# Turning q and k two heads at a time and splitting them afterwards in a hybrid encoder layer

## The chip, the cores and the metric

The kernel runs on one core of one Trainium2 chip. The time is the device time of one execution in microseconds (us); three runs of the kernel before gave 1966.2 to 1967.8 us, with a median of 1966.9 us. The engines are named as in the profile: PE (TensorE), PEld (its weight loads), DVE (VectorE), ACT (ScalarE), POOL (GpSimd) and SP (SyncE, which issues all DMA transfers of this kernel). L885 is line 885 of the kernel.

## The reference, cut to what matters

One layer of a hybrid encoder over 1024 tokens of width 1024: a gated feed-forward block, then attention beside a state-space scan, then a second feed-forward block and a gated embedding. The change touches only the way from the projected q and k to the scores of the attention:

```python
u = x @ w_in[i]
q, k, v, z, xs, bm, cm, dt_raw = jnp.split(u, SPLIT_POINTS, axis=-1)
qf = _rms(q.reshape(B, S, N_Q_HEADS, HEAD_DIM).astype(jnp.float32), q_norm[i])
kf = _rms(k.reshape(B, S, N_KV_HEADS, HEAD_DIM).astype(jnp.float32), k_norm[i])
qh = _apply_rope(qf, cos, sin).astype(x.dtype)
kh = _apply_rope(kf, cos, sin).astype(x.dtype)
...
s = jnp.einsum('bqhgd,bkhd->bhgqk', qi, k, preferred_element_type=jnp.float32) * scale
```

There are eight q heads and two k heads of 64 values each. Behind the attention's inputs come the channels of the scan (`xs`, `bm`, `cm`), which go through a five-tap convolution along the tokens, and `dt_raw`, which goes through a softplus.

## The kernel before, in words

All products keep float32 accuracy by splitting each operand into a high part in the PE's reduced float32 format and a low part, the remainder; `mm3` makes three products of the parts. The scores use the same idea in another form. A head has only 64 values, while a matmul takes 128 partitions, so the high part of a q head lies on partitions 0 to 63 of the tile `Q` and its low part on partitions 64 to 127. `K` holds, for each of the two k heads, a plane with the high part on both halves and a plane with the low part on both halves. Two matmuls of 128 partitions then make all four products of parts.

`in_proj` runs `qkv_part` and then `xbc_part`. In `qkv_part` there are eight token tiles of 128 tokens for q (`qq`, 24 matmuls of 512 columns each) and then eight tiles for k, v and dt together (`kv`, 24 matmuls of 272 columns each). Each result goes through `norm` (ACT squares, DVE sums, POOL takes the power -0.5) and `rope` (L847: a Newton step, the scaling L852, two half products L858, L859 and the sum L860, all on DVE). `step` staggers this by hand: while the product of tile t is issued, `rope` is issued for tile t-1 and the turn of tile t-3 for q. After `rope` the kernel before copies the high part on ACT (L895 for q, L878 for k), subtracts for the low part on DVE (L87, written to the tile `qs`), turns 128 tokens x 128 values with both parts of one head per transpose on PE (L901, eight per q tile; L884, four per k tile, each k part written twice for the two halves), and copies the turned tile from PSUM to `Q` (L902) or `K` (L885) on ACT.

The PE runs strictly in program order (`in_order`). The orders on the other engines and on SP's queue come from a planner that simulates the timeline with costs of its own; each engine then executes its list in order, and a waiting instruction holds what stands behind it.

PSUM is held in two pools: `sm`, four buffers of 512 values, and `big`, two of 1024. The products of q and of k, v, dt stand in `sm`; the turned q tiles of the kernel before stand in `big`, the turned k tiles in `sm`. The work tiles of `qkv_part` (`sq`, `qn`, `qs`) belong to the pool `qwork`. It is closed when `qkv_part` ends, and the pools of `xbc_part` (`xwork` with the tile `conv`, `prep`, `zwork2`, `xtab` with the convolution's table `cw`) take over its addresses.

At the end of `qkv_part` the last steps are not run at once: they are put on `self.pend`, and the first product of the convolution's channels, `xbc_gemm(0)`, made inside `qkv_part`, runs two of them after each of its two halves of 24 matmuls. Then `xbc_part` begins: `cw` is loaded (L957), the products of the channel groups j = 1, 2, ... follow, 48 matmuls each into a buffer of `big`, and each is read by `conv` (one ACT instruction at L964 that needs `cw`, four taps on DVE at L969). `ssd_prep` (L1059 on) works on dt beside it. Group j = 2 needs the `big` buffer that the convolution of group 0 reads.

Of the kernel before, what the change touches and what calls it, by code (L numbers as in the profile page):

```python
# [18 lines left out]
P = 128  # L19
# [17 lines left out]
class Layer:  # L37
# [778 lines left out]
    def qkv_part(self, c, xT):  # L816
# [30 lines left out]

        def rope(v, nh, m, ss, r, nm, t):

            self.newton(r, ss, nh)  # L850
            qn = wk.tile([P, nh, HD], F32, name="qn")
            nc.vector.tensor_tensor(out=qn, in0=v, in1=r.unsqueeze(2).broadcast_to([P, nh, HD]), op=ALU.mult)  # L852
            T1, T2 = (x[:, t] for x in T[nm])
            H2 = HD // 2
            for a in range(2):
                o = slice(a * H2, (a + 1) * H2)
                i = slice((1 - a) * H2, (2 - a) * H2)
                nc.vector.tensor_tensor(out=m[:, :, o], in0=qn[:, :, i], in1=T2[:, o].unsqueeze(1).broadcast_to([P, nh, H2]), op=ALU.mult)  # L858
            nc.vector.tensor_tensor(out=qn, in0=qn, in1=T1.unsqueeze(1).broadcast_to([P, nh, HD]), op=ALU.mult)  # L859
            nc.vector.tensor_tensor(out=qn, in0=qn, in1=m, op=ALU.add)  # L860
            return qn

        NK = NKV * HD
        late = []

        def kv_front(t, ps):
# [5 lines left out]
            return st  # L872

        def kv_back(t, st):

            kn = rope(*st, "k", t).unsqueeze(2).broadcast_to([P, NKV, 2, HD])
            kd = wk.tile([P, NKV, 2, 2, HD], F32R, name="qs", bufs=4)
            nc.scalar.copy(out=kd[:, :, 0], in_=kn)  # L878

            def turn():  # L880
                pt = self.pss().rearrange("p (g j t) -> p g j t", g=NKV, j=2)
                for g in range(NKV):
                    for j in range(2):
                        nc.tensor.transpose(out=pt[:, g, j], in_=kd[:, g, j].rearrange("p a d -> p (a d)").bitcast(F32), identity=self.ident)  # L884
                nc.scalar.copy(out=K[:, :, :, t * P:(t + 1) * P], in_=pt)  # L885
            late.append(turn)
            return kd[:, :, 1], kn, kd[:, :, 0]

# [3 lines left out]
        def q_back(t, st):  # L892
            qs = wk.tile([P, NQ, 2, HD], F32R, name="qs", bufs=4)
            qn = rope(*st, "q", t)
            nc.scalar.copy(out=qs[:, :, 0], in_=qn)  # L895

            def turn():
                pt = self.psb().rearrange("p (h t) -> p h t", t=P)
                qv = qs.bitcast(F32)
                for hh in range(NQ):  # L900
                    nc.tensor.transpose(out=pt[:, hh], in_=qv[:, hh].rearrange("p a d -> p (a d)"), identity=self.ident)  # L901
                nc.scalar.copy(out=Q[:, :, t * P:(t + 1) * P], in_=pt)  # L902
            late.append(turn)
            return qs[:, :, 1], qn, qs[:, :, 0]

        backs, los = [], []

        def step(t, ps, front, back, keep=1):


            if len(late) > keep or not front:
                late.pop(0)()
            st = front(t, ps) if front else None
            if los:
                self.lo(*los.pop())
            if backs:
                los.append(backs.pop()())
            if front:
                backs.append(lambda: back(t, st))

# [6 lines left out]
        for t in range(NT):  # L927
            ps = self.kv(t, xT)
            step(t, ps, kv_front, kv_back, 2)
            if t == 0:  # L930
                tables("k", 1.0)
        self.pend += [lambda: step(NT, None, None, None)] * 4
        self.x0 = self.xbc_gemm(0, xT, 1)
# [1025 lines left out]
```

## Time and profile before

| | us |
|---|---|
| median of three runs | 1966.9 |
| span of the profiled execution | 1962.3 |
| what lies around the span (median less span) | 4.6 |
| PE busy | 1938.6 (99%) |
| DVE busy | 1533.1 (78%) |
| ACT busy | 879.7 (45%) |
| q and k part, start of the first and of the last transpose | 720.3 and 789.5 |

The profiled execution's own time is given as its span alone; the three runs were not profiled, and the difference between their median and the span is taken for what lies around it. Times in the views are counted from the start of the span. In the timeline a row gives the start, the length, the engine, the line, the operation and, in brackets, the idle time before it and what ended it; neighbours of one kind are merged. Matmuls overlap, so a PE row is longer than the distance to the next one.

### The profile page before, as it was taken

What the parts mean: (1) busy time and instruction counts of PE and PEld (TensorE: products, weight loads), DVE (VectorE), ACT (ScalarE), POOL (GpSimd) and SP (SyncE); (2) the same over time, 40 slices, a digit from 0 to 9 for tenths busy, and PEclk for the clock granted to TensorE, in tenths of its full rate; (3) what the DMA queues carried; (4) which work ended last, traced back from release to release, by engine and by line L of the source; (5) the groups of instructions that cost most, each with busy time, mean ns of one, the idle gap of its engine ahead of it and who ended that gap; (6) DMA issues with size and microseconds to landing.
All of it is one profiled execution on the core that took longest, in us unless ns stands there. A gap on an engine that the chain in (4) does not pass through costs nothing.

```text
span 1962.3 us, 25749 instructions
## 1 busy us (share of the span) xinstructions
PE 1938.6 (99%) x9196; PEld 1614.3 (82%) x9196; DVE 1533.1 (78%) x2378; ACT 879.7 (45%) x1509; POOL 392.8 (20%) x292
## 2 busy tenths in 40 slices
PE   8999999999999999999999999999999999999998
PEld 7888888888888889888888888788888888888886
DVE  7977776867668658759998878997777777787698
ACT  7433333334444224538887775643333334443311
POOL 0144544430001132000101001003545440001011
PEclk9999999999999999999999999999999999999999
DMA  8434544559865112231003383253545439986122
GB/s 303 136 124 154 192 177 145 193 187 377 282 226 172 65 42 68 87 111 45 7 1 98 116 292 114 86 179 138 185 146 202 159 135 336 341 267 220 39 75 97
DMA packets 147180, 309.95 MB, mean 158 GB/s; under 512 B 17665, under 2 KB 30337, under 8 KB 147052
## 3 DMA queue, kind: packets, MB, share of 16 engines
q1 hardware_dynamic: 147052, 308.31, 44.9%
q8 instruction: 72, 1.18, 0.3%
q14 instruction: 56, 0.46, 0.1%
HBM read 216.83 MB, written 91.42 MB: 157 GB/s over the span
## 4 chain that ended last, share of the span: by engine, by line
PE 90%; DVE 6%; DMA 1%; POOL 1%; issue 1%; ACT 1%; SPq 0%; DVEq 0%; ACTq 0%; POOLq 0%
PE sm L122 56%; PE big L508 12%; PE sm L508 9%; PE big L122 3%; PE big L1151 2%; PE sm L1173 2%; DVE nm L1158 1%; PE sm L1188 1%; PE sm L1189 1%; POOL qr L845 1%; PE sm L1366 1%; PE sm L1262 1%; PE sm L1273 1%; DVE ptl L87 1%; DVE xl L87 1%
## 5 line engine op out<-in xcount | busy, mean ns | idle before, releaser
L122 PE MATMUL sm<-xh,blk 128*128 128x512 f32 x1424 | 439.9, 389 | 0.0
L122 PEld LDWEIGHTS sm<-xh,blk 128*128 128x128 f32 x1424 | 267.3, 188 | 55.4
L122 PE MATMUL sm<-xl,blk 128*128 128x512 f32 x736 | 283.9, 389 | 3.8 <-DVE xl L87 3.8
L122 PE MATMUL sm<-blk,xl 128*128 128x512 f32 (+2 forms) x784 | 238.4, 371 | 0.9 <-DVE qn L852 0.5
L122 PE MATMUL sm<-blk,xh 128*128 128x512 f32 (+2 forms) x584 | 202.7, 379 | 0.0
L108 ACT CAST blk<-raw 128x512 fp32r<-128x512 f32 (+1 forms) x168 | 101.1, 610 | 213.2 <-PE sm L122 128.6
L87 DVE TENSOR_TENSOR blk<-s,blk 128x512 fp32r<-128x512 f32 x176 | 152.1, 869 | 35.4 <-ACT blk L108 34.3
L87 DVE TENSOR_TENSOR blk<-raw,blk 128x512 fp32r<-128x512 f32 (+1 forms) x168 | 145.8, 871 | 37.9 <-ACT blk L108 37.5
L108 ACT CAST blk<-s 128x512 fp32r<-128x512 f32 x172 | 105.7, 622 | 138.9 <-PE sm L122 122.3
L122 PEld LDWEIGHTS sm<-xl,blk 128*128 128x128 f32 x736 | 138.2, 188 | 32.7 <-issue 4.2
L122 PEld LDWEIGHTS sm<-blk,xl 128*128 128x128 f32 x784 | 142.9, 188 | 25.3 <-PE sm L884 0.8
L178 POOL TENSOR_TENSOR ln_k<-ln_k,mhalf 128x1 f32<-128x1 f32 x32 | 36.9, 1158 | 583.2 <-DVE ln_k L177 578.2
L508 PE MATMUL big<-xh 128*128 128x512 f32 x576 | 138.8, 390 | 0.0
L267 POOL TENSOR_TENSOR s<-raw 128x512 f32<-128x512 f32 x34 | 55.1, 1621 | 387.4 <-DVE blk L87 294.3
L87 DVE TENSOR_TENSOR xh<-blk,xh 128x1024 fp32r<-128x1024 f32 x78 | 95.4, 1223 | 47.0 <-ACT xh L454 39.2
L454 ACT CAST xl<-blk 128x1024 fp32r<-128x1024 f32 x76 | 80.1, 1054 | 114.0 <-PE sm L508 43.2
L454 ACT CAST xh<-blk 128x1024 fp32r<-128x1024 f32 x78 | 82.2, 1054 | 106.7 <-PE big L508 47.4
L508 PEld LDWEIGHTS big<-xh 128*128 128x128 f32 x576 | 107.8, 188 | 22.2
L87 DVE TENSOR_TENSOR xl<-blk,xl 128x1024 fp32r<-128x1024 f32 x76 | 92.6, 1219 | 42.6 <-ACT xl L454 36.5
L122 PEld LDWEIGHTS sm<-blk,xh 128*128 128x128 f32 x584 | 109.8, 188 | 19.2
L508 PE MATMUL big<-xl 128*128 128x512 f32 x480 | 115.8, 390 | 0.0
L122 PE MATMUL sm<-xET3h,blk 128*128 128x512 f32 x352 | 108.4, 389 | 0.0
(339 smaller groups left out, 4025.3 us busy)
## 6 DMA issues: line engine op xcount, KB each, us to landing
raw<-in_wi_dram SPq DMA_DIRECT2D x81, 512.0 KB
blk<-hS SPq DMA_DIRECT2D x154, 256.0 KB
hS<-h SPq DMA_DIRECT2D x88, 256.0 KB
wr<-in_wo_dram SPq DMA_DIRECT2D x44, 512.0 KB
blk<-wT SPq DMA_DIRECT2D x88, 256.0 KB
hS<-sg SPq DMA_DIRECT2D x66, 256.0 KB
wT<-wr SPq DMA_DIRECT2D x66, 256.0 KB
blk<-in_wo_dram SPq DMA_DIRECT2D x66, 256.0 KB
```

Of the source, the lines that this page charges most:

```text
L87: (eng or self.nc.vector).tensor_tensor(out=out, in0=full, in1=hi.bitcast(F32), op=ALU.subtract)
L108: self.nc.scalar.copy(out=b[:, 0, :n], in_=src)
L122: self.nc.tensor.matmul(ps, lhsT=a, rhs=b, start=(i == 0), stop=(i == n - 1))
L178: nc.gpsimd.tensor_tensor(out=r, in0=v, in1=self.mhalf[:, :1], op=ALU.pow)
L267: lambda: G.tensor_tensor(out=s1, in0=a21, in1=a22, op=ALU.add),
L454: A.copy(out=b[:, :, 0], in_=r)
L508: nc.tensor.matmul(ps[q], lhsT=b[:, 0, x, cut], rhs=b[:, 1, y], start=j == i == 0, stop=j == NP - 1 and i == 2)
L845: nc.gpsimd.tensor_tensor(out=r, in0=ss, in1=self.mhalf[:, :nh], op=ALU.pow)
L1151: nc.tensor.matmul(ps[:, n * 512:(n + 1) * 512], lhsT=Q[:, h, q0:q0 + P], rhs=K[:, h // 4, j, n * 512:(n + 1) * 512], start=j == 0, stop=j ...
L1158: nc.vector.tensor_reduce(out=nm, in_=ps, axis=AX.X, op=ALU.max, negate=True)
L1173: nc.tensor.transpose(out=pt[:, k], in_=pr[:, kk * P:(kk + 1) * P], identity=self.ident)
L1188: nc.tensor.matmul(po, lhsT=vw, rhs=pth[k // 4][:, k % 4], start=k == 0, stop=False)
```

## The change

q and k leave `rope` as plain float32 values. Two heads (128 values) of one tile are turned by one transpose: four transposes for a q tile; k tiles are gathered four at a time in `kn`, and the two k heads of a tile make one transpose, four for each half of the tokens. The new function `turned` puts the four results in one `sm` buffer. ACT copies the high part from there to `qhi`, DVE subtracts for the low part to `qlo`, and DMA transfers on SP's queue bring the parts of both heads to their partitions of `Q` and `K`: four transfers for a q tile (64 partitions x 4 runs of 512 bytes), eight for a half of k (64 partitions x one run of 2048 bytes). For the odd head of a pair the order of the two parts on the partitions is exchanged; since `K` has the same part on both halves, the scores stay the same. `qs` and its copies on ACT and DVE go. In the k part the turns stand at other steps: q tiles 5, 6 and 7 are turned in steps 0, 1 and 2 of the k part (before, in steps 1, 2 and 3), the first half of k in step 5, and the second half in the last pending steps, behind the second half of `xbc_gemm(0)`.

```diff
-        def rope(v, nh, m, ss, r, nm, t):
+        def rope(qn, v, nh, m, ss, r, nm, t):
 
             self.newton(r, ss, nh)
-            qn = wk.tile([P, nh, HD], F32, name="qn")
             nc.vector.tensor_tensor(out=qn, in0=v, in1=r.unsqueeze(2).broadcast_to([P, nh, HD]), op=ALU.mult)
...
-            return qn
 
         NK = NKV * HD
-        late = []
+        late, backs, los = [], [], []
+
+        def turned(blocks, place):
+
+            pt = self.pss()
+            for i, b in enumerate(blocks):
+                nc.tensor.transpose(out=pt[:, i * P:(i + 1) * P], in_=b, identity=self.ident)
+            hi, lo = (wk.tile([P, 512], F32R, name=n) for n in ("qhi", "qlo"))
+            nc.scalar.copy(out=hi, in_=pt)
+
+            def rest():
+                self.lo(lo, pt, hi)
+                for j, part in enumerate((hi, lo)):
+                    for e in range(2):
+                        for out in place(e, j):
+                            nc.sync.dma_start(out=out.bitcast(F32), in_=part[e * HD:(e + 1) * HD].bitcast(F32))
+            los.append(rest)
...
+        kn = {}
+
         def kv_back(t, st):
 
-            kn = rope(*st, "k", t).unsqueeze(2).broadcast_to([P, NKV, 2, HD])
-            kd = wk.tile([P, NKV, 2, 2, HD], F32R, name="qs", bufs=4)
-            nc.scalar.copy(out=kd[:, :, 0], in_=kn)
-
-            def turn():
-                pt = self.pss().rearrange("p (g j t) -> p g j t", g=NKV, j=2)
-                for g in range(NKV):
-                    for j in range(2):
-                        nc.tensor.transpose(out=pt[:, g, j], in_=kd[:, g, j].rearrange("p a d -> p (a d)").bitcast(F32), identity=self.ident)
-                nc.scalar.copy(out=K[:, :, :, t * P:(t + 1) * P], in_=pt)
-            late.append(turn)
-            return kd[:, :, 1], kn, kd[:, :, 0]
+            h = t // 4
+            if t % 4 == 0:
+                kn[h] = wk.tile([P, 4, NKV, HD], F32, name="kn")
+            rope(kn[h][:, t % 4], *st, "k", t)
+            if t % 4 == 3:
+                cols = slice(h * 512, (h + 1) * 512)
+                late.append(lambda: turned([kn[h][:, i].rearrange("p g d -> p (g d)") for i in range(4)],
+                                           lambda g, j: [K[r * HD:(r + 1) * HD, g, j, cols] for r in range(2)]))
 
         def q_front(t, ps):
             return norm(ps, NQ)
 
         def q_back(t, st):
-            qs = wk.tile([P, NQ, 2, HD], F32R, name="qs", bufs=4)
-            qn = rope(*st, "q", t)
-            nc.scalar.copy(out=qs[:, :, 0], in_=qn)
-
-            def turn():
-                pt = self.psb().rearrange("p (h t) -> p h t", t=P)
-                qv = qs.bitcast(F32)
-                for hh in range(NQ):
-                    nc.tensor.transpose(out=pt[:, hh], in_=qv[:, hh].rearrange("p a d -> p (a d)"), identity=self.ident)
-                nc.scalar.copy(out=Q[:, :, t * P:(t + 1) * P], in_=pt)
-            late.append(turn)
-            return qs[:, :, 1], qn, qs[:, :, 0]
-
-        backs, los = [], []
+            qn = wk.tile([P, NQ, HD], F32, name="qn", bufs=4)
+            rope(qn, *st, "q", t)
+            Qv = Q.rearrange("p (i e) s -> p i e s", e=2)[:, :, :, t * P:(t + 1) * P]
+
+            def place(e, j):
+                r = e ^ j
+                return [Qv[r * HD:(r + 1) * HD, :, e]]
+            late.append(lambda: turned([qn[:, 2 * i:2 * i + 2].rearrange("p h d -> p (h d)") for i in range(4)], place))
 
         def step(t, ps, front, back, keep=1):
 
-
-            if len(late) > keep or not front:
+            if len(late) > keep:
                 late.pop(0)()
-            st = front(t, ps) if front else None
+            st = front(t, ps)
             if los:
-                self.lo(*los.pop())
+                los.pop()()
             if backs:
-                los.append(backs.pop()())
-            if front:
-                backs.append(lambda: back(t, st))
+                backs.pop()()
+            backs.append(lambda: back(t, st))
...
-            step(t, ps, kv_front, kv_back, 2)
+            step(t, ps, kv_front, kv_back, 1 if t < 2 else 0)
...
-        self.pend += [lambda: step(NT, None, None, None)] * 4
+        self.pend += [lambda: backs.pop()(), lambda: None, lambda: late.pop()(), lambda: los.pop()()]
```

## The prediction, made before the changed kernel was run

> **What bounds the kernel now.** I read the page first, then the busy time of each engine by stretches of the q and k part, the chain of waits there, the timeline, and SP's waits.
>
> ```profile
> span 1962.3 us, 25749 instructions
> PE 90%; DVE 6%; DMA 1%; POOL 1%; issue 1%; ACT 1%; SPq 0%; DVEq 0%; ACTq 0%; POOLq 0%
> ```
>
> The span is a chain of PE work for 90%. So PE time that is removed counts in full, unless something that PE waits for does not move with it.
>
> ```profile
> 732.00:744.00 12.00, 12.00 (x62) 10.10 (x62) 9.82 (x26) 5.11 (x8) 4.12 (x2) 1.00 0.01 2
> 744.00:756.00 12.00, 11.89 (x90) 11.30 (x90) 9.60 (x30) 6.61 (x13) 4.97 (x2) 1.00 0.48 154
> 756.00:766.50 10.50, 9.37 (x76) 8.94 (x76) 9.86 (x44) 4.21 (x12) 2.12 (x3) 1.00 0.01 3
> 766.50:778.00 11.50, 11.47 (x89) 11.33 (x90) 10.82 (x56) 6.50 (x18) 2.86 (x4) 1.00 0.03 6
> ```
>
> After the length the columns are busy us of PE, PEld, DVE, ACT and POOL, then the granted clock (1.00 throughout). PE is full in the q part, but DVE is at 80 to 94%, and where q passes into k PE idles 0.11 + 1.13 + 0.03 = 1.27 us: there DVE is the one waited for.
>
> **The change part by part.**
>
> Transposes. The chain gives eight of them as one piece, and four as another:
>
> ```profile
> 769.78 0.44 PE sm L884 x4
> 782.62 0.88 PE sm L884 x8
> L901 PE MATMUL big<-ident,qs x64: 270/273/301, 720.3 to 762.3; 128*128 128x128 f32 x64
> ```
>
> A transpose takes 0.11 us of PE's time in a row of them, though its own record is 0.273 us long. q goes from 64 to 32, k from 32 to 8: 56 x 0.11 = 6.2 us of PE work less. The Trainium skill, "TensorE: Matmul & The Clock Gate", Part 4 (PE-mode transpose), gives about 275 ns for one in a kernel; as a saving that would be 56 x 0.275 = 15.4 us. The record agrees with the page, the spacing does not, and the spacing is what PE pays.
>
> Copies. ACT loses, per q tile, the copies L895 and L902, and per k tile L878 and L885; DVE loses L87 on `qs`. Instead come, per turned block, one ACT and one DVE instruction of 512 values from PSUM, for which the last turn before q has the rows:
>
> ```profile
> L902 ACT CAST Q<-big 128x1024 fp32r<-128x1024 f32 x8 | 8.1, 1015 | 0.6 <-PE big L901 0.5
> L87 DVE TENSOR_TENSOR qs<-qn,qs x16: 415/549/693, 716.4 to 787.5; 128x512 fp32r<-128x512 f32 x8, 128x256 fp32r<-128x256 f32 x8
> 698.71 0.59 ACT L228 CAST xl<-big 128x512 fp32r<-128x512 f32 x1 [0.23 <-PE big L224]
> 700.67 0.69 DVE L87 TENSOR_TENSOR xh<-big,xl 128x512 fp32r<-128x512 f32 x1 [0.65 <-ACT xl L228]
> ```
>
> For q, DVE stays as it is (0.69 each); for k it falls from 8 x 0.42 to 2 x 0.69 us, 2.0 us less. ACT has slack either way. None of this is PE time; it counts only where PE waits for DVE.
>
> That place is q tile 7:
>
> ```profile
> 744.83 0.33 SPq L94 DMA_DIRECT2D raw<-in_wkv_dram  x1
> 748.20 0.59 ACT L840 ACTIVATE sq<-sm 128x512 f32<-128x512 f32 x1
> 751.42 3.21 POOL L845 TENSOR_TENSOR qr<-ss,mhalf 128x8 f32<-128x8 f32 x1 [5.12 <-DVE ss L843]
> 759.04 0.68 DVE L860 TENSOR_TENSOR qn<-qn,sq 128x512 f32<-128x512 f32 x1
> 761.47 1.06 PE L901 MATMUL big<-ident,qs 128*128 128x128 f32 x8 [0.61 <-DVE qs L87]
> 766.53 0.36 PE L122 MATMUL sm<-blk,xl 128*128 128x272 f32 x1 [0.55 <-DVE qn L852]
> ```
>
> Its `rope` ends at 759.04 + 0.68 = 759.72, and its transposes wait until 761.47 for the ACT copy and L87 behind it. After the change they need only L860, but they stand one k tile earlier. PE would arrive there early: the transposes of tiles 0 to 6 save 7 x 0.44 = 3.1 us, and one k tile (3.04 us in the row below) now follows instead of leading; 761.47 - 0.61 = 760.9, less 3.1 and 3.0, is 754.8. So PE now waits for `rope` of tile 7, and the question is how far L860 moves ahead. Not at all is the one bound (its sum, square and power hang on ACT's order, on POOL and on the transfer of `wkv`, which now shares SP's queue with the transfers of q). The other bound is no wait at all. Tile 7's product ends 4 x 0.44 = 1.7 us earlier, and the copy L895, which held ACT's list until L860 of the tile before, is gone; with up to 1.2 us for that I take 2.3 us, nearer the row's 1.7.
>
> ```profile
> 770.22 3.04 PE sm L122 x24
> 777.14 5.47 PE big L122 x24
> 788.79 1.03 PE L884 MATMUL sm<-ident,qs 128*128 128x128 f32 x8
> ```
>
> From L860 to the end of group 0's product PE then has: 0.2 for the signal (an estimate), the turn 0.44, possibly 0.4 until `rope` of k tile 0 frees an `sm` buffer (as at 766.53; the turned blocks now share these four), five k tiles 5 x 3.04 = 15.2, a turn 0.44, two halves 10.9: 27.2 to 27.6 us. Before it is 788.79 - 759.72 = 29.07. The product of group 0 so ends 2.3 + 1.7 = 4.0 us earlier; with L860 unmoved 1.7, with no wait at all 6.9 (8 q turns 3.5 + six k turns 2.6 - one new 0.44 + the 1.27 us of stalls).
>
> The transfers. 8 x 4 + 2 x 8 = 48 are added, 128 KB each, on a queue that is nearly empty. Those of q have until the attention to land, and the weights of the convolution's groups are loaded ahead, so I cost them at nothing; without that cover they are 48 x 0.48 = 23 us of SP's time. The last eight are the exception. `qwork` must be free before anything of `xbc_part` may touch its addresses, and today's rows show that wait:
>
> ```profile
> SPq L957 <- PE sm L884: 1.8, 1, 1.8
> 789.85 0.33 SPq L957 DMA_DIRECT2D cw<-in_cw_dram  x1
> 790.23 0.42 SPq L784 DMA_DIRECT2D pa<-in_a_log_dram  x1
> 790.71 0.42 SPq L1082 DMA_DIRECT2D tri<-in_tri_dram  x1
> 792.38 1.19 ACT L964 ACTIVATE conv<-big,cw 128x1024 f32<-128x1024 f32 x1
> 797.72 1.28 DVE L969 SCALAR_TENSOR_TENSOR conv<-big,cw,conv 128x1022 f32<-128x1022 f32 x1
> 698.51 2.00 DMA zd<-z
> 744.83 2.65 DMA raw<-in_wkv_dram
> 702.44 5.61 DMA ws_q<-in_qns_dram
> ```
>
> The load of `cw` has no data from the turns, yet it waits for the last L884, the last reader of `qwork`, and goes out 1.06 us after 788.79. The convolution starts 3.59 us after 788.79 and is done at 799.0, 10.2 us after. Now the last readers are transfers. From the end T of group 0's product: transposes 0.44, ACT copy until 1.25, L87 until 2.0, eight issues 0.48 apart (790.23 to 790.71) from 1.35 on, so the last goes out at 4.7. No row shows a transfer from SBUF to SBUF; nearest in size (256 and 272 KB) are 2.00 and 2.65 us, and 5.61 is the slowest here (256-byte rows spread over partitions). I take 2.0 to 2.65: landed at 6.7 to 7.4. Then `cw` goes out and needs 2.0 to 2.5 (789.85 to 792.38): the convolution starts at T + 8.8 to 9.9 instead of T + 3.6, 5.2 to 6.3 later, and with it `ssd_prep`, which takes over the same addresses. Behind the waiting `cw` on SP stand `pa`, `tri` and one weight load for a group not needed yet.
>
> The Trainium skill, "SBUF — State Buffer", Door 1 (the DMA port swizzle), says that 64 partitions reach half of the ports and gives 196 GB/s for 1 MiB. By it an estimate for the eight transfers (1 MiB) is 5.3 us from 1.35 on, landed by about 7.2 with a little for completion; that leaves the sum as it is. No run here shows it.
>
> PE does not wait for the convolution at once: group 1's product covers it.
>
> ```profile
> 814.80 10.91 PE big L122 x48
> 813.91 0.30 PE sm L1111
> ```
>
> Group 2 needs the buffer that convolution 0 reads. Before, PE gets there at 788.79 + 0.87 + 10.91 = 800.57, 11.78 after T, and the buffer is free at 10.2: 1.6 us to spare. After, PE gets there at T + 11.35, and the buffer is free at T + 15.4 to 16.5: a stall of 4.1 to 5.2 us. Against before, group 2 starts 15.4 to 16.5 - 11.78 = 3.6 to 4.7 us later relative to T. Further on the ACT and DVE chain up to L1111 is tight already (PE is back to unbroken products at 814.80, after that wait), which can add the rest of the convolution's delay, up to about 1.4; I take 0.5.
>
> **The sum** against the profiled execution: -4.0 + 4.2 + 0.5 = +0.7 us. Its span becomes 1963.0, and with the 4.6 us by which the median of the runs shown (1966.9) exceeds the span, the time 1967.6. Ends: -6.9 + 3.6 = -3.3 (1963.6) and -1.7 + 4.7 + 1.4 = +4.4 (1971.3).
>
> **The rivals.**
>
> The gain stays. Were the addresses handed over with no wait for the transfers, or PE's order covered it, the convolution would start as now after T. Four transposes fewer stand between groups 0 and 1 (0.44), so -4.0 - 0.44 = -4.4: 1962.5, at most -7.3: 1959.6. For it speaks the 90% of PE; against it the row in which `cw` waits for L884.
>
> Slower: `rope` of tile 7 does not move. DVE and POOL are not relieved for q, POOL's 3.21 us and the transfer of `wkv` stay, and PE stands still before k tile 3 instead of behind it. Then the lead at T is 1.7, and with 4.7 and 1.4 the time is 1971.3. It ends beyond 0.2% when L860 moves by less than about 0.5 us and the release comes at its late end. For it: DVE's 80 to 94%. Against it: tile 7's product is 1.7 us earlier by PE's work alone.
>
> Slower: the transfers land as late as the slowest row. 5.61 instead of about 2.3 puts the release, the convolution and the stall 3.3 us later: 1967.6 + 3.3 = 1970.9. It decides from a landing of 5.6 us on. Against it: that row is made of pieces of 256 bytes, these are of 2048.
>
> Transposes cost their record. 56 x 0.273 = 15.3 us saved, less the same late release: 1966.9 - 15.3 + 4.7 = 1956.3. Against it are the 0.88 us for eight, and DVE would not follow anyway.
>
> **How the numbers follow.** A difference within 0.2% (3.9 us: 1963.0 to 1970.8) can't be told from no change here. The forecast has 0.50, all within. The gain that stays has 0.14 (0.10 faster, 0.04 same), the unmoved `rope` 0.22 (0.16 slower, 0.06 same), the late landing 0.11 (0.07 slower, 0.04 same), the dear transposes 0.03, faster. Faster 0.13, same 0.64, slower 0.23. The range reaches a little into the cases on both sides, 1962.6 to 1971.6; the likeliest case alone spans 1963.6 to 1970.
>
> **What would show it.** The chain should hold 32 + 8 transposes at 0.11 us. PE should be idle 1 to 3 us before the transposes of q tile 7, released by L860; if it is idle for none, or for 5, the lead at T is off as bounded. The load of `cw` should go out 6.7 to 7.4 us after group 0's product ends, not 1, and the first L964 some 2.3 us after that. PE should show a wait of 4 to 5 us for L969 before group 2, where none stands now. If the release comes at once, or the planner finds an order in which group 2 does not wait, the prediction is wrong towards faster; if SP's queue holds the loads of `wkv` or the turns of k behind a waiting transfer, towards slower.

## The result, and the profile after

The changed kernel is slower. Its median is 1979.3 us (five runs, 1977.5 to 1980.7) against 1967.8 us (1966.2 to 1968.1) for the kernel before on the same chip: a ratio of 1.0062 with a 95% interval of 1.0050 to 1.0074. The prediction was 1967.6 us, with a range from 1962.6 to 1971.6. So the time lies 11.7 us above the forecast and 7.7 us beyond the range.

The span of the profiled execution goes from 1962.3 to 1975.7 us, 13.4 us more. PE makes up 91% of the chain of waits, 90% before: an average over 1976 us does not show where 12 us went. The waits of PE show it. This view lists, between 600 and 1000 us, what PE stood still for (total, count, longest):

```profile
PE big L122 <- DVE conv L973: 9.6, 1, 9.6
PE sm L122 <- DVE blk L87: 2.4, 1, 2.4
PE sm L122 <- DVE qn L851: 1.1, 1, 1.1
PE sm L122 <- DVE kn L851: 0.8, 1, 0.8
PE sm L868 <- DVE qn L859: 0.6, 1, 0.6
```

The lines of the changed kernel stand four higher behind `qkv_part`, so L973 is a tap of the convolution (L969 before). One wait of 9.6 us is most of the loss. The busy time by stretches adds a second thing (columns as before: PE, PEld, DVE, ACT, POOL, then the granted clock):

```profile
744.00:756.00 12.00, 9.45 (x62) 8.81 (x60) 10.24 (x29) 3.87 (x9) 4.37 (x2) 0.86 0.72 185
802.00:814.00 12.00, 3.85 (x9) 3.10 (x10) 11.87 (x18) 4.48 (x6) 0.00 (x0) 0.65 0.14 44
814.00:826.00 12.00, 11.82 (x56) 9.58 (x55) 2.95 (x9) 4.22 (x6) 0.00 (x0) 0.93 0.00 1
```

The granted clock, 1.00 in the q and k part before, falls to 0.86 where q passes into k, and to 0.65 and 0.93 around the stall.

To compare kernels whose q part starts at slightly different times, I count from the start of ACT's first square of q. Before and after these rows stand at the start and the end of the stage (ACT's square, the last turn of k, the last of the turns behind L1111, which is L1115 now; the last turn of k is T of the prediction, and its row of before, at 788.79, stands there):

```profile
704.16 0.60 ACT L840 ACTIVATE sq<-sm 128x512 f32<-128x512 f32 x1 [3.52 <-PE sm L122]
814.50 0.30 PE L1111 MATMUL sm<-ident,ldt 128*64 128x128 f32 x1
```

```profile
704.30 0.60 ACT L840 ACTIVATE sq<-sm 128x512 f32<-128x512 f32 x1 [3.52 <-PE sm L122]
789.06 0.60 PE L868 MATMUL sm<-ident,kn 128*128 128x128 f32 x4
810.15 0.76 PE L122 MATMUL big<-xh,blk 128*128 128x512 f32 x1 [9.59 <-DVE conv L973]
826.79 0.30 PE L1115 MATMUL sm<-ident,ldt 128*64 128x128 f32 x1
```

From the first square to T: 788.79 - 704.16 = 84.63 before, 789.06 - 704.30 = 84.76 after, so no lead at all (+0.13). From T to the start of group 2: 800.57 - 788.79 = 11.78 before, 810.15 - 789.06 = 21.09 after (+9.31). From there to the end of the stage: 814.80 - 800.57 = 14.23 before, 827.09 - 810.15 = 16.94 after (+2.71). The sum is +12.15 us, and the timed difference is 11.5.

The chain of waits of the changed kernel goes through these places, with other pieces between them (start, length, engine or transfer, line):

```profile
745.35 3.03 DMA raw<-in_wkv_dram
752.28 5.19 DMA Q<-qlo
790.38 0.47 SPq L877
794.73 2.35 DMA K<-qlo
798.12 1.28 ACT L1065
801.72 1.19 DVE conv L973
```

The eight K transfers go out one after another from 790.38 on, the last at 794.73; that one lands at 797.1, and only then do the table load on ACT for `prep` (L1065) and the convolution begin. SP's queue and ACT say the same:

```profile
792.82 2.51 SPq L877 DMA_DIRECT2D K<-qlo  x4
795.37 0.59 SPq L94 DMA_DIRECT2D raw<-in_wx_dram  x1
797.30 0.33 SPq L961 DMA_DIRECT2D cw<-in_cw_dram  x1
800.15 1.20 ACT L968 ACTIVATE conv<-big,cw 128x1024 f32<-128x1024 f32 x1
```

`cw`, which has nothing to do with k, goes out 797.30 - 789.06 = 8.2 us after T instead of 1.06, and the convolution begins 11.1 us after T instead of 3.6.

### The profile page after: what moved, and what is told of

Read it like the earlier page. It is cut to its first block, busy times and chain, and to the rows that moved or that the text cites. A ratio compares the mean times of both kernels' runs of the same rounds, so it can differ in the third digit from the quotient of the medians.

```text
span 1975.7 us, 25688 instructions
## 1 busy us (share of the span) xinstructions
PE 1938.9 (98%) x9140; PEld 1613.8 (82%) x9140; DVE 1531.0 (77%) x2372; ACT 864.2 (44%) x1486; POOL 393.6 (20%) x292
## 4 chain that ended last, share of the span: by engine, by line
PE 91%; DVE 6%; DMA 1%; issue 1%; POOL 1%; ACT 1%; SPq 0%; DVEq 0%; ACTq 0%; POOLq 0%
PE sm L122 56%; PE big L508 12%; PE sm L508 9%; PE big L122 3%; PE big L1155 2%; PE sm L1177 2%; DVE nm L1162 1%; PE sm L1192 1%; PE sm L1193 1%; PE sm L1370 1%; PE sm L1266 1%; PE sm L1277 1%; POOL qr L845 1%; DVE ptl L87 1%; DVE xl L87 1%
## 5 line engine op out<-in xcount | busy, mean ns | idle before, releaser
L122 PE MATMUL sm<-xET2h,blk 128*128 128x512 f32 x352 | 108.5, 390 | 0.0
```

The lines of the kernel that those rows point to most:

```text
L122: self.nc.tensor.matmul(ps, lhsT=a, rhs=b, start=(i == 0), stop=(i == n - 1))
```

## The experiments

Each is the changed kernel with one edit, unless said otherwise. They carry numbers and are grouped by what they ask. The line numbers shift by a few from kernel to kernel. "T" and "stage" are times from the first square of q to T and to the end of the second turn of `ldt`, read as above.

**Is the late release the cause of the stall?** Experiment 1 gives k's parts a pool of their own that stays open through `xbc_part`, so that no transfer reads `qwork` at its end.

```diff
+        self.kparts = parts.enter_context(tc.tile_pool(name="kparts", bufs=1))
         with ExitStack() as c2:
             self.qkv_part(c2, xT)
...
-            hi, lo = (wk.tile([P, 512], F32R, name=n) for n in ("qhi", "qlo"))
+            hi, lo = (pool.tile([P, 512], F32R, name=n) for n in ("qhi", "qlo"))
```

> One edit to the changed kernel: the split parts of k stand in a pool of their own that stays open until the end of the convolution part, so nothing of that part waits for the last eight transfers. Theory (late release): the load of cw goes out about 1 us after the last transposes of k as in the kernel before, the 9.6 us stall ahead of channel group 2 goes to 0 to 0.5 us, and with it the 2.9 us that group 2 lost at half clock: 12.3 us faster than the changed kernel, about 1967 us. Rival (the convolution is late by the planner's order on DVE, which mixes the taps of groups 0 and 1, not by the release): a stall of 3 us or more stays, 1973 us or more.

Measured: 1965.3 us, ratio to the kernel before 0.9997 (0.9988 to 1.0007). From SP's queue and from PE:

```profile
787.20 0.60 PE L871 MATMUL sm<-ident,kn 128*128 128x128 f32 x4
787.83 0.33 SPq L964 DMA_DIRECT2D cw<-in_cw_dram  x1
788.73 2.38 SPq L880 DMA_DIRECT2D K<-qhi  x4
```

`cw` goes out 0.63 us after the last turn, ahead of the K transfers; the wait before group 2 is gone, and the clock stays at 1.00 there. The kernel is 14.0 us faster than the changed one, where 12.3 were expected. Part of that lies ahead of the stall: T is 787.20 - 704.67 = 82.53, 2.2 us earlier than in the changed kernel. Experiments 13 to 16 come back to this.

Experiment 9 changes q alone; k is copied, split and turned as in the kernel before.

```diff
-            h = t // 4
-            if t % 4 == 0:
-                kn[h] = wk.tile([P, 4, NKV, HD], F32, name="kn")
-            rope(kn[h][:, t % 4], *st, "k", t)
...
+            kd = wk.tile([P, NKV, 2, 2, HD], F32R, name="qs", bufs=4)
+            nc.scalar.copy(out=kd[:, :, 0], in_=kn)
```

> The change for q alone; k is copied, split and turned as in the kernel before. By the theory that only k's last transfers hold the buffers, cw is loaded about 1 us after T, there is no stall of more than 1 us before group 2 and the clock stays at 1.00 there. The lead is that of the first experiment (1.6 us) less k's 24 transposes (2.6 us) plus 0.4 for the one turn of k that goes: T some 0.6 us later than before the change, 1967.3 us, between 1966 and 1968.5. If q's transfers hold the buffers too, a stall of several us remains and the time is above 1972.

Measured: 1969.7 us, ratio 1.0014 (1.0005 to 1.0024). No stall stands before group 2, and `cw` goes out at once again:

```profile
792.58 1.03 PE L902 MATMUL sm<-ident,qs 128*128 128x128 f32 x8
793.65 0.33 SPq L968 DMA_DIRECT2D cw<-in_cw_dram  x1
756.00:766.50 10.50, 8.02 (x49) 7.59 (x50) 8.15 (x34) 1.76 (x6) 2.09 (x3) 0.84 0.93 195
```

So the stall belongs to k's half of the change. The time missed its interval, though: T is 792.58 - 704.80 = 87.78, 3.15 us later than before instead of 0.6. PE waits at the entry to k again, and the third row shows a clock of 0.84 there. q's half alone gains nothing.

**What is the 9.6 us made of?** Experiment 5 puts `cw` in a tile of its own, loaded early; experiment 10 lets DVE take the taps of conv 1 only behind all four of conv 0; experiment 11 does both.

```diff
-        cw = tabs.tile([P, 8, 6], F32, name="cw")
-        nc.sync.dma_start(out=cw, in_=I["cw"])
+        cw = self.cw
...
+                    self.tc.add_manual_dep(one, end0.name, mybir.DependencyInfo(mybir.DependencyClass.NoSync, mybir.DependencyReason.DATA), reason="in_order")
```

> The changed kernel, with the convolution's table cw in a tile of its own that is loaded long before, so that no load stands between the last K transfer and the first convolution. If release plus load is the chain that sets the stall, the first conv on ACT starts about 2 us earlier (T + 9 instead of T + 11.1, T being the end of group 0's product) and the stall before group 2 falls from 9.6 to about 7.5 us: 1977.2 us by the stall alone, and down to 1976 if the shorter stall also loses less to the clock. If instead the work tiles' release and the mixing of the taps of conv 0 and conv 1 on DVE set it, the stall stays above 9 us and the time at 1979.

> The changed kernel with one order imposed: the taps of conv 1 on DVE come behind all four taps of conv 0. If the two taps of conv 1 that DVE ran in between are a part of the stall before group 2, it falls by 2.4 us (two taps of 1.19), from 9.6 to about 7.2, and the time to 1976.9 us; more than that if the clock drops for less long. If the stall is the late release alone, it stays at 9.6 and the time at 1979.3.

> The same order of the taps and, as in the fifth experiment, cw in a tile of its own, loaded early. If late release, the load of cw behind it and the mixed taps are three separate parts of the stall, the two savings add: 9.6 - 2.3 - 2.4 = 4.9 us are left, within the 4.1 to 5.2 us that the prediction had for the release alone, and the time is 1974.6 us with the clock dropping as before, about 1972 without. If they share a part, the stall stays near 7.

Measured: 1978.4 us (ratio 1.0055, 1.0038 to 1.0072), 1977.6 us (1.0056, 1.0040 to 1.0073) and 1975.3 us (1.0044, 1.0029 to 1.0059). PE's row at the start of group 2 in the fifth and in the tenth (in the eleventh the wait is 6.15):

```profile
810.61 0.76 PE L122 MATMUL big<-xh,blk 128*128 128x512 f32 x1 [7.33 <-DVE conv L974]
```

```profile
808.02 0.77 PE L122 MATMUL big<-xh,blk 128*128 128x512 f32 x1 [7.25 <-DVE conv L973]
```

The load of `cw` and its place on ACT (the convolution now runs ahead of the table load for `prep`) are worth 9.59 - 7.33 = 2.3 us of the stall, the two taps of conv 1 that DVE ran in between 9.59 - 7.25 = 2.3. Together they give 3.4, not 4.6 (4.9 us was expected to be left, and 6.15 are): in the eleventh kernel DVE puts a reciprocal of `prep` and a second split of weights among the taps instead. The time of the fifth did not follow the shorter stall, since its PE stood 4.5 us, not 2.4, for the weights of k; T came 1.9 us later.

**And the rest, behind the stall?** Experiment 2 puts 40 matmuls that nobody reads before group 2, so that PE is busy while it would wait.

```diff
+                if j == 2:
+                    d = self.pss()
+                    for i in range(40):
+                        self.nc.tensor.matmul(d, lhsT=xT[0][0][0][:, 0, :P], rhs=xT[0][0][0][:, 0], start=True, stop=True)
```

> The changed kernel with 40 extra matmuls of 512 columns (9.1 us, result unused) ahead of channel group 2, inside the 9.6 us in which PE stood still. Theory (an idle PE is given a lower clock): the granted clock stays 1.00, group 2 takes 10.9 us instead of 13.8, and the kernel is about 2.9 us faster than the changed one, 1976.4 us, although PE has more to do. Rival (group 2 is slow for another reason, or the stall only moves): no difference, 1979 us, or slower.

Measured: 1976.6 us, ratio 1.0056 (1.0041 to 1.0071). Group 2 in the chain of waits of the changed kernel, and then the same and the stretch of the stall in experiment 2:

```profile
810.15 13.77 PE big L122 x48
```

```profile
810.96 11.18 PE big L122 x48
802.00:814.00 12.00, 11.51 (x51) 9.23 (x50) 11.97 (x18) 4.64 (x7) 0.00 (x0) 1.00 0.14 45
```

With PE kept busy the clock stays at 1.00, and the 48 matmuls take 11.2 us instead of 13.8 (10.91 before). PE gets to group 2 no sooner, 810.96 - 789.87 = 21.09 us after T as without them. So the idle time costs a second time: 13.77 - 10.91 = 2.86 us of slow matmuls behind it.

**Where did the lead at T go?** Five kernels ask this one item at a time. Experiment 6 gives `qhi` and `qlo` three buffers in the changed kernel, with the order of all engines the same; experiment 4 does so in the kernel of experiment 1, and 7 is the same kernel as 4 again.

```diff
-            hi, lo = (wk.tile([P, 512], F32R, name=n) for n in ("qhi", "qlo"))
+            hi, lo = (wk.tile([P, 512], F32R, name=n, bufs=3) for n in ("qhi", "qlo"))
```

> The first edit (parts of k apart) and three instead of two buffers for each of the split parts of q. In the changed kernel the subtraction for q tile 6 waits until a transfer of tile 4's low part has landed, 5.2 us after its issue. Theory (slow landing holds DVE and through it PE): the wait of DVE for that transfer goes, rope of tile 7 ends 0.5 to 1.5 us earlier, and so does group 0's product: 1965.5 to 1966.5 us. Rival (DVE has other work to do first, or the wait for the wkv load decides): same as the first edit alone within 0.5 us.

> The changed kernel with three buffers each for qhi and qlo; the order of instructions on every engine and queue is the same. If the reuse of two part buffers behind slow landings is what ate the lead, T moves from 789.06 to about 787, and, since the stall of 9.6 us before group 2 stays, the time is 1979.3 - 2.0 = 1977.3 us. If the lead was eaten by the late last third of wkv (2.4 us of idle PE and the lower clock behind it), T moves by less than 0.5 us and the time stays at 1979.

> The fourth experiment's kernel (k's parts in a pool of their own, three buffers for q's) once more, for a narrower interval: 1963.7 us, 0.9985 to 0.9993 of the time before if its gain is real; an interval that holds 1.000 if it was scatter.

Measured: experiment 4 1963.7 us (0.9989, 0.9979 to 0.9998), with T at 80.36; experiment 6 1978.5 us (1.0060, 1.0045 to 1.0075), with T at 83.75; experiment 7 1962.2 us (0.9980, 0.9971 to 0.9989), with T at 80.35. The same edit is worth 2.2 us of T in one kernel, more than the 0.5 to 1.5 expected, and 1.0 in the other, less than the 2 expected.

Experiments 3 and 12 load the last third of `wkv` early into a tile of its own, 3 in the kernel of experiment 1, 12 in that of experiment 6.

```diff
+        self.wkv_raw = tabs.tile([P, 544], F32, name="wkvr")
+        nc.sync.dma_start(out=self.wkv_raw, in_=I["wkv"][:, 6 * 272:])
```

> The first edit (parts of k apart) and, beside it, a tile of its own for the last third of the weights of k, v and dt, loaded ahead, so that PE no longer waits 2.4 us for it in the first k tile. Theory A (that late load took the lead that PE had from the fewer transposes): the wait goes, the half clock behind it too, and the product of channel group 0 ends 3 to 4 us earlier than with the first edit alone, about 1963.5 us. Theory B (DVE's chain up to the rope of q tile 7 sets the entry to k): PE only gets earlier to the transposes of tile 7 and waits there 3 us or more; 0 to 1.5 us faster than the first edit alone, 1965.5 to 1967 us.

> The changed kernel with three buffers each for qhi and qlo and a tile of its own for the last third of wkv, loaded early; k's parts stay in qwork. If the lead at T was eaten by the late last third of wkv (2.4 us of idle PE, and the lower clock behind it) and by the two part buffers, and by nothing else, T counted from the start of q's first square is 80.4 us (as in the fourth experiment; 84.6 before, 84.8 in the changed kernel), while the stall of 9.6 us before group 2 stays: 1979.3 - 4.3 = 1975.0 us. If DVE's order alone made k's weights late, PE still waits over 2 us for blk at L87, T stays above 83 and the time above 1977.5.

Measured: experiment 3 1964.7 us (0.9992, 0.9982 to 1.0001), the same as experiment 1 within the intervals, with T 0.3 us earlier; the wait of 3 us before tile 7 that its second theory named did not come (0.4 us). Experiment 12 1981.2 us (1.0070, 1.0053 to 1.0087). It refutes the first of its theories, and of the second only the numbers came true: the wait for the weights of k is gone, and yet T is later (88.40). Waits for `sm` buffers that DVE has not read yet (2.5, 1.4 and 1.3 us) have taken its place. PE waits for DVE as a whole there, and taking one item away only names the next. Experiment 8 asks for the `sm` buffers: it puts q's turned blocks in `big` in the kernel of experiment 4.

```diff
-            pt = self.pss()
+            pt = self.psb()[:, :512] if pool is wk else self.pss()
```

> The same kernel with q's turned blocks in a big PSUM buffer instead of one of the four sm buffers. If the three waits of 0.6 to 0.8 us for sm buffers in the k part come from the turned blocks that share them, two of these go and T moves from 785.1 to about 783.6: 1962.2 us. If PE only meets the next wait (rope of the same tile on DVE), T moves by less than 0.5 us and the time is the same, 1963.7.

Measured: 1964.5 us (0.9988, 0.9980 to 0.9997) beside 1962.2 for experiment 7, with T 0.3 us earlier; why the time is longer all the same was not looked into. The waits for `sm` go, and PE waits 1.3 us for `rope` of tile 7 instead: again DVE.

Why is DVE later in one kernel than in another? Rows of the start of the q part in the changed kernel, on SP and on DVE, answer that:

```profile
692.28 6.68 SPq L1021 DMA_DIRECT2D zd<-z  x2
700.77 0.33 SPq L823 DMA_DIRECT2D cs<-in_cs_dram  x1
708.05 0.69 DVE L834 SCALAR_TENSOR_TENSOR T<-sn,ws_q 128x512 f32<-128x512 f32 x1 [0.49 <-DMA ws_q<-in_qns_dram]
714.97 0.69 DVE L859 TENSOR_TENSOR qn<-qn,sq 128x512 f32<-128x512 f32 x1
```

SP waits with the load of `cs` until `zd<-z` has landed (1.6 us in the list of SP's waits), though the two share no data: the tables of q lie on addresses that the transfers of `zd` still read. `cs` and the norm weights are loaded only when those are done, 3.5 us before the first square, and the sum of `rope` of tile 0 starts 714.97 - 704.30 = 10.67 us after that square (10.83 before). In experiment 1 the additional pool shifted the addresses, `cs` was loaded some 123 us earlier (at 578.0), and the sum starts after 7.40 us. So experiments 1, 3, 4, 7 and 8 had changed two things. Experiment 13 shifts the addresses alone, by an unused pool of the same size; 14 does so in the kernel before; 15 is experiment 4 once more beside it; 16 adds three buffers to 13.

```diff
+        sp = parts.enter_context(tc.tile_pool(name="kparts", bufs=1))
+        for n in ("sp0", "sp1"):
+            sp.tile([P, 512], F32R, name=n)
```

> The changed kernel with an unused pool of the size of k's part tiles (4 KB a partition) where the first experiment had them; k's parts stay in qwork. With it cs, sn and the norm weights are loaded long before the q part, as in the first experiment, and rope of q tile 0 ends about 3.3 us earlier after the start of q's first square (7.4 instead of 10.7 us). If this shift of addresses is what gave the first experiment its lead, T counted from the first square is 82.5 us (84.8 in the changed kernel), while the stall of 9.6 us before group 2 stays: 1979.3 - 2.2 = 1977.1 us. If the lead came from k's parts lying apart, T stays at 84.8 and the time at 1979.3. If the shift of addresses also took the stall away, the time is 1965 and the late release is not the cause.

> The kernel before with the same unused pool. If the early tables are worth what PE waits between q and k before (0.11 + 1.13 + 0.03 = 1.27 us) and nothing else, the time is 1966.5 - 1.2 = 1965.3 us, and of the gain of the fourth and seventh experiments (2.8 to 4.3 us) the rest, 1.6 to 3.1 us, belongs to the change. If nothing depends on them, it stays at 1966.5; if they are worth the 3.3 us in full, it is 1963.2 and the change is worth nothing even without the stall.

> The fourth experiment's kernel on the same chip as the kernel before with the unused pool: 1962.2 to 1963.7 us as before. Its distance to that kernel is what the change is worth once its stall is gone: 4.3 - 1.3 = 3.0 us less if both give what they gave, none if the early tables are the whole gain.

> The changed kernel with the unused pool (early tables) and three buffers each for qhi and qlo; k's parts stay in qwork. If the lead at T needs these two and nothing else, T counted from the first square is 80.3 us, as in the fourth, seventh and fifteenth runs (84.66 with the pool alone, 83.75 with the buffers alone), and with the stall of 9.6 us still there the time is 1979.3 - 4.4 = 1974.9 us. If the lead also needs k's parts to lie apart, T is nearer 83 and the time above 1976.5.

Measured, with the runs of before in this table for comparison:

| kernel | tables of q | part buffers for q | k's parts apart | T, us | stall before group 2, us | median, us | ratio (95% interval) |
|---|---|---|---|---|---|---|---|
| before | late | - | - | 84.63 | 0 | 1967.8 | 1 |
| 14: before, shifted | early | - | - | 82.71 | 0 | 1964.7 | 0.9995 (0.9986 to 1.0004) |
| changed | late | 2 | no | 84.76 | 9.6 | 1979.3 | 1.0062 (1.0050 to 1.0074) |
| 6 | late | 3 | no | 83.75 | 9.6 | 1978.5 | 1.0060 (1.0045 to 1.0075) |
| 13 | early | 2 | no | 84.66 | 9.6 | 1977.0 | 1.0055 (1.0041 to 1.0069) |
| 16 | early | 3 | no | 80.42 | 9.6 | 1975.1 | 1.0046 (1.0029 to 1.0062) |
| 1 | early | 2 | yes | 82.53 | 0 | 1965.3 | 0.9997 (0.9988 to 1.0007) |
| 15 (as 4 and 7) | early | 3 | yes | 80.28 | 0 | 1963.4 | 0.9984 (0.9975 to 0.9993) |

Each ratio is against runs of the kernel before on the same chip (medians 1966.4 to 1967.8). The rows for T and the stall in experiment 16:

```profile
704.23 0.60 ACT L845 ACTIVATE sq<-sm 128x512 f32<-128x512 f32 x1 [3.52 <-PE sm L122]
784.65 0.60 PE L873 MATMUL sm<-ident,kn 128*128 128x128 f32 x4
805.77 0.76 PE L122 MATMUL big<-xh,blk 128*128 128x512 f32 x1 [9.61 <-DVE conv L978]
```

Experiment 16 came out as expected, in T (80.42 for 80.3) and in time (1975.1 for 1974.9). In the profiled executions the lead needs the early tables and the third pair of buffers together; either alone gives 1.0 us or less while k's parts lie in `qwork`. With both, k's parts apart change nothing in T (80.42 and 80.28), but take away the stall: 1975.1 - 1963.4 = 11.7 us.

For the early tables alone this is less firm. Experiment 13 came out as expected in time (1977.0 for 1977.1) but not in T (84.66 for 82.5). Its four runs fall in two pairs, 1975.0 and 1975.6 us and 1978.5 and 1978.8, and T was read from one of the second pair, with the lower clock of the two (0.993 against 0.994 and 0.995). Experiment 1, with two buffers too, is 2.1 us ahead of it at T. The thirteenth waits longer for `rope` of tile 7, and the clock falls behind that wait (the first's rows, then the thirteenth's):

```profile
PE sm L871 <- DVE qn L862: 2.1, 1, 2.1
756.00:766.50 10.50, 7.56 (x60) 7.13 (x59) 9.98 (x46) 1.89 (x7) 2.11 (x3) 1.00 0.71 153
```

```profile
PE sm L873 <- DVE qn L864: 2.8, 1, 2.8
756.00:766.50 10.50, 6.90 (x42) 6.47 (x42) 8.27 (x35) 1.46 (x5) 1.42 (x2) 0.84 0.64 147
```

The longer wait (0.7 us) and the lost clock (10.5 x 0.16 = 1.7 us at most) are of the size of those 2.1 us. So the early tables alone give between nothing and some 2 us at T; the runs do not settle it more closely.

Experiment 14 corrects what experiments 4 and 7 seemed to say. The kernel before gains 1.92 us at T from the early tables alone, more than the 1.27 us that PE idled there; with them PE no longer waits at all in this part. (The 0.65 us beyond that idle time lie in PE's busy time, 83.36 to 82.71 us at the same clock; why it is shorter was not looked into.) Against that kernel the change without its stall is worth 82.71 - 80.28 = 2.43 us at T, and 2.6 us at the end of the stage (106.10 against 108.73). In time it is 1964.7 - 1963.4 = 1.3 us. The two intervals against the kernel before overlap, but both kernels ran on the same chip, and ten of the eleven runs of experiment 15 (1961.8 to 1963.5 us, the other at 1965.9) are faster than the fastest of the eleven of experiment 14 (1963.95). So the change without its stall is worth a little, 1 to 3 us.

## Why the prediction was wrong, point by point

**The transposes** were right. One piece of four is still 0.44 us in the chain (771.84, on L868), and L868 has 32 transposes for q and 8 for k.

**The lead at T** was the first step that failed. It was to be 4.0 us (2.3 by an earlier L860 of tile 7 and 1.7 behind it), from 1.7 to 6.9, and T came 0.13 later, outside its bounds. The part of it that went by PE's own work was right: the product of tile 7 ends 1.7 us earlier, as predicted (the turn right behind it starts 744.11 - 704.30 = 39.81 us after the first square instead of 745.65 - 704.16 = 41.49), and its square follows 42.47 us after the first square instead of 44.04. But L860, now L859, of tile 7 did not follow by 2.3 us. Rows of the changed kernel:

```profile
746.77 0.60 ACT L840 ACTIVATE sq<-sm 128x512 f32<-128x512 f32 x1 [4.50 <-DVE rs_t L129]
755.75 0.17 DVE L881 TENSOR_TENSOR dt<-sm,dtb 128x16 f32<-128x16 f32 x1 [1.20 <-PE sm L122]
757.59 0.69 DVE L87 TENSOR_TENSOR qlo<-sm,qhi 128x512 fp32r<-128x512 f32 x1 [0.32 <-DMA Q<-qlo]
760.27 0.69 DVE L859 TENSOR_TENSOR qn<-qn,sq 128x512 f32<-128x512 f32 x1
```

L859 starts 55.97 us after the first square, against 759.04 - 704.16 = 54.88 before: 1.1 us later. From its end to T PE then needed 28.1 us (29.07 before, 27.2 to 27.6 predicted), so that 1.0 of the 1.7 us came. The bound "not at all" was no bound, since DVE could fall behind too. Between the steps of this `rope`, DVE's list has an addition for k's dt, which stood 1.20 us for a product that PE made late, and a low part of q, which stood 0.32 us for a transfer.

On PE the account from the first square to T closes. The rows are before, changed, and experiment 15, which has the same PE instructions there with the clock at 1.00:

```profile
704.16:788.79 84.63, 83.36 (x497) 73.85 (x496) 67.49 (x229) 34.12 (x71) 22.61 (x16) 1.00 0.15 49
704.30:789.06 84.76, 79.72 (x445) 69.71 (x444) 65.20 (x222) 20.94 (x50) 22.46 (x16) 0.98 0.44 110
705.56:785.84 80.28, 78.30 (x444) 68.26 (x443) 64.03 (x220) 21.35 (x50) 21.89 (x16) 1.00 0.48 115
```

The fewer transposes take 83.36 - 78.30 = 5.06 us off PE's work (3.5 + 2.6 - 0.44 = 5.7 by the prediction). PE stands still for 84.76 - 79.72 = 5.04 us instead of 1.27, and the lower clock costs 79.72 - 78.30 = 1.42 us: 5.06 - 3.77 - 1.42 = -0.13. The longest of the waits, 2.4 us, is for the weights of k, which DVE has to split first; PE stood only 0.6 us before the turn of tile 7, where the prediction looked for 1 to 3.

The step of the prediction that failed here is "Those of q have until the attention to land", for which they were costed at nothing. The attention is not the only one that waits for a transfer out of SBUF: the next low part in the same buffer waits too, and it stands on DVE's list ahead of `rope`. The chain passes through one such landing, 5.19 us for `Q<-qlo`, amid weight loads of 512 KB. Three buffers alone, with the same order on all engines, give 1.0 us back; with early tables they give 4.24 in the profiled executions (84.66 to 80.42). The early tables are the second half: the row for `ws_q` with its 5.61 us, from which the prediction took a bound for another transfer, was itself the sign that DVE starts the q part late. By which of DVE's waits the two buffers cost that much is not shown.

The 4.0 us are near what the change gives once DVE is not held up, 84.63 - 80.28 = 4.35 at T, but that is chance: 1.92 of it is owed to the early tables, which the change does not bring.

**The late release** was right as a mechanism and mis-sized by about half. Predicted was a start of group 2 3.6 to 4.7 us later relative to T; it is 9.31. Term by term, from T: the issues start at 1.32 (predicted 1.35) but stand 0.62 us apart on average, not 0.48, so that the transfers have landed at 8.0, not 6.7 to 7.4. `cw` goes out at 8.2, and from there to the convolution 2.85 us pass instead of 2.0 to 2.5, while ACT runs the table load for `prep` and a split of weights first. So the convolution starts at 11.1 instead of 8.8 to 9.9. The largest term is the last: conv 0 holds its buffer for 10.0 us instead of 6.6, because DVE runs two taps of conv 1 and one more split of weights in between; the prediction had carried the 6.6 over. Experiments 5 and 10 take 2.3 us each off the stall, by the early `cw` and by the order of the taps. The common fault is this: the durations were taken from a stage in which conv 1 came behind conv 0 (792.38 and 801.34 on ACT before). Released late, both start almost at once (800.15 and 801.35), and DVE's list puts two taps of conv 1 ahead of the last ones of conv 0, whose buffer PE needs.

**The clock** was not in the sum at all, neither in the lead (1.42 us above) nor behind the stall. The whole difference behind the start of group 2, +2.71 (predicted +0.5 at L1111), is group 2 itself at 13.77 instead of 10.91 us, less 0.15 elsewhere; experiment 2 shows that it goes away when PE is kept busy. The Trainium skill, "TensorE: Matmul & The Clock Gate", Part 1 (the HAM clock gate), states that PE falls to half rate after at least one idle window of about 3.4 us and needs as long of work to come back. The stretch from 802 to 814 us, with its granted clock of 0.65, agrees that it falls; the stretch from 744 to 756 us, with 0.86, holds no wait longer than 2.4 us, and a wait of 3.8 us left the clock at 1.00 in one execution (below). By these traces the length of one wait does not decide it. The prediction priced a stall of 4 to 5 us and should have asked what such a stall does to the work behind it.

**The sum** by these steps: forecast +0.7, to which come 4.1 for the lead, 9.31 - 4.2 = 5.1 for the release and 2.71 - 0.5 = 2.2 for the clock behind the stall, 12.1 in all, against 12.15 in the trace.

**The rivals.** The unmoved `rope` was the nearest: DVE was not relieved, but PE stood for k's weights and for `sm` buffers more than before tile 7, and the rival was capped at a lead of 1.7. Late landing did not come where it was placed: K's last part landed in 2.35 us; it was one of q's that took 5.19. The gain that stays and the dear transposes did not occur.

**The time around the span.** The prediction added 4.6 us, the median less the span of the profiled execution. The profiled execution of the changed kernel took 1977.5 us for a span of 1975.7, 1.8 us around it, and in the timed runs of the kernel before beside the experiments it is 1.8 to 1.9 too, with spans from 1962.6 to 1966.9. So the profiled execution of before, with 1962.3, was faster than all of these, and the other 2.7 us of the 4.6 are scatter between executions. A difference of two spans carries such scatter (13.4 here, 11.5 timed). Part of it can be seen: far behind the stage PE has the same wait for DVE in both kernels (a row and the stretch around it, before, then changed).

```profile
1267.87 0.47 PE L122 MATMUL sm<-xl,blk 128*128 128x512 f32 x1 [3.80 <-DVE xl L87]
1262.00:1269.00 7.00, 3.20 (x15) 2.36 (x14) 6.25 (x12) 1.92 (x4) 0.00 (x0) 1.00 0.05 8
```

```profile
1279.81 0.65 PE L122 MATMUL sm<-xl,blk 128*128 128x512 f32 x1 [3.80 <-DVE xl L87]
1276.00:1283.00 7.00, 3.20 (x9) 2.58 (x9) 7.00 (x13) 2.64 (x5) 0.00 (x0) 0.78 0.31 103
```

The clock fell in one profiled execution and not in the other, and from this row to the end of the span it is 1975.7 - 1279.81 = 695.9 us instead of 1962.3 - 1267.87 = 694.4. That is 1.5 us that the change did not cause: experiment 14, the kernel before but for its pool, has the wait too, with a clock of 0.82 in the same stretch.

## What to carry to other kernels

When a tile is read by a transfer instead of an engine, its buffer, and the pool that it lies in, come free a queue, an issue and a landing later; look for who takes over the buffer or the addresses, and keep parts that are transferred at the end of a stage in a pool that outlives it. A stall of PE is priced with the slow matmuls behind it, and work that a late release sets free all at once is not done in the order, or in the time, in which it was done before. An experiment that adds a pool also moves addresses: run the unused pool alone, in both kernels, before its gain is credited to anything else.

## What the runs showed of the hardware that was not expected

- The granted clock went down while PE stood idle (and not when matmuls filled that time) and came back only some 5 us into the work: 0.62 from 804 to 810 us and 0.50 from 810 to 814, where the matmuls already run. The price was 2.86 us for 9.59 us of idling.

```profile
804.00:810.00 6.00, 0.00 (x0) 0.00 (x0) 6.00 (x9) 0.00 (x0) 0.00 (x0) 0.62 0.28 87
810.00:814.00 4.00, 3.85 (x9) 3.10 (x10) 3.87 (x9) 3.44 (x4) 0.00 (x0) 0.50 0.00 0
```

- The length of a single wait did not tell whether the clock falls: 0.86 in the stretch with the 2.4 us wait of the changed kernel, 0.84 in that with the 2.8 us wait of experiment 13, 1.00 in that with the 2.1 us wait of experiment 1, and 1.00, 0.78 and 0.82 around the same wait of 3.8 us in the profiled executions of the kernel before, of the changed one and of experiment 14.
- A transfer of 128 KB from 64 partitions to 64 others landed 2.35 us after its issue as the last of eight in a row, and 5.19 us after it amid weight loads of 512 KB and other transfers of q; no run separates what made the difference. Four such issues take 2.51 us of SP's queue, 0.63 each.
